# Four 64x64 quadrants for the recurrence of a hybrid trunk, a 16x16 block inverse, and shape changes in the planner's costs

## The chip, the cores and the metric

The kernel runs on one core of a Trainium2 chip. A core has TensorE (128 x 128 array, PE in the profile; its weight loads are PEld), VectorE (DVE), ScalarE (ACT), GpSimd (POOL) and SyncE (SP, which issues the transfers). Matrix products read SBUF and write PSUM, which has eight banks of 512 fp32 columns on 128 partitions. The metric is the device time of one execution in microseconds (us), the median of several; lower is better.

## The reference

A trunk of four residual layers on x of 256 tokens x 1024 channels, fp32. Layers 0 and 3 mix tokens with RWKV-7, layer 1 with stick-breaking attention, layer 2 with sparse attention over keys that an indexer selects; a SwiGLU network follows each. The change concerns RWKV-7 (16 heads of 64 channels), whose core is a recurrence over tokens:

```python
def step(state, inp):                      # state: 64 x 64 for each head
    r_t, w_t, k_t, v_t, kk_t, a_t = inp
    sa = jnp.einsum('bhvk,bhk->bhv', state, kk_t)
    state = (state * w_t[:, :, None, :]
             - sa[..., None] * (kk_t * a_t)[:, :, None, :]
             + v_t[..., None] * k_t[:, :, None, :])
    return state, jnp.einsum('bhvk,bhk->bhv', state, r_t)
...
y = ((y - mu) * lax.rsqrt(var + RW_GN_EPS)).reshape(B, S, D) * ln_w + ln_b
y = y + (jnp.sum(rh * kh * r_k, axis=-1, keepdims=True) * vh).reshape(B, S, D)
out = (y * g).astype(h.dtype) @ w_out
```

## The kernel before, in words

Activations lie with channels on partitions: 1024 channels are 8 groups (index p, NC = 8) of 128 partitions, two heads in each. `halves` lists for the two heads hh of a group their own 64 partitions r and the other 64, rb. Functions work on two neighbouring groups at a time, which I call a pair of groups.

The recurrence is cut into chunks of C = 64 tokens, NCH = 4 of them. Inside a chunk it is linear algebra on 64 x 64 blocks for each head. The steps and the names of their buffers, which the profile shows as out<-in:

- `sc`: products of keys and queries of a chunk, masked into SB (strict part for the inverse, the other part for the output).
- the inverse of a unit lower triangular 64 x 64 matrix for each head and chunk. First its two 32 x 32 diagonal blocks are inverted by forward substitution on VectorE: all 256 blocks lie along partitions and the free axis (`blocks`, `inv`), and 31 iterations of a multiply and a subtract each handle 31 to 256 elements a partition. A transposed copy goes to XT. Then `combine` makes the off-diagonal 32 x 32 block with two TensorE units of 16 tiny products (`cmb1`, `cmb2`) for each pair of groups; `xd` is a transposed copy of XT that it needs.
- `vp`: the product that makes the values, 128 single fp32 products of 256 columns over both layers, ends in `vfirst`. `qct`: transposes of keys. `vtok`: values turned to tokens on partitions and centred, into UV. `bv`: SB times UV, the part of the right-hand side that does not depend on the state.
- `bn`: sums over a head's channels by a product with a block matrix of ones (`bonesr`), in two products of split fp32 (`prhl`, split by `exact`).
- `pg`: the gate.
- `Chain`: one for each pair of groups, two of them alternate, for groups 0 to 3 and then 4 to 7. A step c does: pS = state times PR (four 64x64 products); u = pS + BV on VectorE; Y<-PR,Sn (the state's part of the output); xu = XT times u; UV = -xu (scaling on ScalarE or VectorE); qu = QC times UV (K = 128, four products of 128 x 64 tiles); the new state Sn = (qu) dc + (Sp dc), the second term made as Sd; Y<-SB,UV (K = 128).
- `post`: the output's group norm, and `po`, the output projection.

A head's products use the 64 x 64 part of the array with rows r (or rb) and columns r: two heads of a group take two of the four quadrants.

The order of the work is not the order of the code. A `Plan` records every operation; `unit(at_once, ns)` binds TensorE products into one piece of work with a given cost. A list scheduler (`_schedule`) then sets for each engine the order, by ranks from the longest remaining path, by a table of perturbations of ranks (`NUDGES`) and by a cost `SWITCH` for a change between products that use half the array or less and whole-array products. Where TensorE would stand idle, `keep_warm` inserts bf16 products into an unused bank (`warm_o`, "warmers"). Operations of queue `anye` may go to ScalarE or VectorE. All recorded instructions are issued from one helper line (L788 before, L808 after); the warmers have their own (L1893, L1933). `bank` takes one of the PSUM banks, `t1` and `t2` take rotating SBUF buffers of 256 and 512 columns.

The core of the substitution:

```python
for i in range(31):
    shape = [P, 31 - i, i + 1]
    ...
    dve.tensor_tensor(t, a, b, op=ALU.mult)
    dve.tensor_tensor(XI[:, i + 1:, :i + 1], XI[:, i + 1:, :i + 1], t, op=ALU.subtract)
```

Of the kernel before, what the change touches and what calls it, by code (L numbers as in the profile page):

```python
# [22 lines left out]
P = 128  # L23
# [14 lines left out]
LAST = 4  # L38
NEG = -1.0e30
# [21 lines left out]


# [118 lines left out]
class Op:  # L181


    def __init__(self, eng):
        self.eng, self.instrs, self.cost, self.table, self.cols = eng, [], 0.0, None, 0.0
        self.preds, self.succs, self.alts, self.warmer, self.parts = set(), [], {}, False, False
# [68 lines left out]
SWITCH = 95.0  # L255
# [53 lines left out]
class Plan:  # L309
# [37 lines left out]
    def record(self, eng, method, args, kw):  # L347
# [19 lines left out]
        if eng == "tensor":  # L367
            op.cols += _columns(method, outs[0], ins)
            op.parts = outs[0].p1 - outs[0].p0 <= 64 or ins[0].p1 - ins[0].p0 <= 64
# [101 lines left out]
    def _schedule(self, counts, reserve):  # L471
        engines = ("tensor", "vector", "scalar", "gpsimd", "sync")
        ready, pending, free = ({e: v() for e in engines} for v in (list, list, float))
        out, recent, parts = [], collections.deque(), False
# [68 lines left out]
        def keep_warm(t, until):  # L543

            nonlocal parts, hot
# [14 lines left out]
            t, parts = t + (SWITCH if parts else 0.0), False  # L560
# [25 lines left out]
        def choose(e, t):  # L586
# [3 lines left out]
            while ready[e] and got is None:  # L590
# [17 lines left out]
                if watch and o.parts != parts and held is None and not o.alts:  # L608
                    held = item, r[1]
                    skipped.append(item)  # L610
                    continue
                if held and (o.parts != parts or o.rank < held[0][2].rank - STICK):
# [20 lines left out]
        while done < len(self.ops):  # L633
# [132 lines left out]
    def emit(self, nc, counts, warmer):  # L766
# [12 lines left out]
        for k in sorted(first, key=lambda k: size[k] % 128 > 0):  # L779
            first[k].get()  # L780
# [11 lines left out]
def trunk(ctx: ExitStack, tc: tile.TileContext, xT_in, vecs_in, wts, lora_in, consts_in, id32_in, nqk_in, outT, order, layers=None):  # L792
# [42 lines left out]
    def consts0():  # L835
        load_consts(0)
        pool.tensor_copy(identb, cst("ident"))
        anye.copy(bonesr, cst("bones"))
# [10 lines left out]
    bonesr = T([P], name="bonesr", dtype=F32R)  # L849
# [53 lines left out]

    def exact(out, w, x, hl):

        split(hl[0], hl[1], x)
        with unit():
            pe.matmul(out, w, hl[0], start=True, stop=False)
            pe.matmul(out, w, hl[1], start=False, stop=True)
# [182 lines left out]
    def rwkv(j, layer, after):  # L1092
# [119 lines left out]
        for p in range(0, NC, 2):  # L1212
            pw = bank("lw"), bank("la")
            with unit(2, 960.0):
# [59 lines left out]
        for p in range(0, NC, 2):  # L1274
# [5 lines left out]
            am = t2("am")  # L1280
            for q in range(2):
                anye.affine(am[:, q], Ft[:, p + q, :], vec(f"ka{j}", p + q), omka[:, j, p + q:p + q + 1])
            dve.tensor_tensor(Et[:, p:p + 2], am, di, op=ALU.mult)
            dve.tensor_tensor(Ft[:, p:p + 2], Ft[:, p:p + 2], di, op=ALU.mult)
# [36 lines left out]
        for p in range(NC):  # L1321
            o = bank("sc"), bank("sc")
            with unit(2):
# [8 lines left out]
        room = T([2, 1024], "s0", "blocks")  # L1332
        ct_ = room[:, 0].rearrange("p (t k a c) -> p t k a c", t=32, k=2, a=4)
        for k in range(2):
            for g in range(4):
                r, b = slice(g * 32, (g + 1) * 32), g % 2
                anye.copy(ct_[r, :, k].rearrange("p t a c -> p a c t"), SB[k][r, g // 2, :, :, 0, b * 32:(b + 1) * 32])
        inv = T([2, 32, 32], "s7", "inv")
        dve.transpose(flat(inv[:, 0]), ct_.rearrange("p t k a c -> p (t k a c)"))
        sp.dma_start(inv[:, 1], id32_in)  # L1340
        ab_, XI = inv[:, 0], inv[:, 1]
        xtmp = room[:, 1, :S]
        for i in range(31):
            shape = [P, 31 - i, i + 1]
            t = xtmp[:, :(i + 1) * (31 - i)].rearrange("p (a b) -> p a b", a=31 - i)
            a = ab_[:, i + 1:, i:i + 1].to_broadcast(shape)
            b = XI[:, i:i + 1, :i + 1].to_broadcast(shape)
            dve.tensor_tensor(t, a, b, op=ALU.mult)
            dve.tensor_tensor(XI[:, i + 1:, :i + 1], XI[:, i + 1:, :i + 1], t, op=ALU.subtract)

        XT = [T([16, C], t, "XT") for t in ("wh", "wl")]
        for k in range(2):
            anye.memset(XT[k], 0.0)
        ct_ = room[:, 0].rearrange("p (t k u) -> p t k u", t=32, k=2)
        dve.transpose(ct_.rearrange("p t k u -> p (t k u)"), flat(inv[:, 1]))
        for k in range(2):
            for g in range(4):
                r, b = slice(g * 32, (g + 1) * 32), g % 2
                anye.copy(XT[k][r, :, b * 32:(b + 1) * 32], ct_[r, :, k].rearrange("p t u -> p u t"))
# [38 lines left out]
        for p in range(0, NC, 2):  # L1398
            o = bank("qct"), bank("qct")
            with unit(2, 560.0):  # L1400
# [9 lines left out]
        for p in range(0, NC, 2):  # L1410
            Vp = vfirst[p // 2]
            o = bank("vtok")
            with unit(1, 990.0):
                for q in range(2):
                    for c in range(NCH):
                        for hh, r, rb in halves:
                            pe.matmul(o[rb, q * S + c * C:q * S + (c + 1) * C], Vp[r, q, c * C:(c + 1) * C],
                                      cst("center")[r, hh * 64:hh * 64 + 64], start=True, stop=True)
            for hh, r, rb in halves:
                anye.copy(UV[hh][rb, p:p + 2].rearrange("p n c t -> p (n c) t"), c8(o[rb, :]))  # L1420
            o = bank("bv")
            with unit(1, 980.0):
                for q in range(2):
                    for c in range(NCH):
                        for hh, r, rb in halves:
                            pe.matmul(o[r, q * S + c * C:q * S + (c + 1) * C], SB[p // 4][rb, hh, p % 4 + q, c, 0, :],
                                      UV[hh][rb, p + q, c, :], start=True, stop=True)
            anye.copy(pairs(BV, p), c8(o))


        for p in range(0, NC, 2):
            prs = t2("prs")
            for q in range(2):
                anye.scale(prs[:, q], pr[:, p + q], vec(f"rk{j}", p + q))
            bn = bank("bn")
            exact(bn, bonesr, flat(prs), [flat(t2("prhl", F32R)) for _ in range(2)])
            dve.tensor_tensor(pr[:, p:p + 2], ab(bn), vfirst[p // 2], op=ALU.mult)
# [14 lines left out]
        def combine(p):  # L1452

            X = XT[p // 4][:, (p % 4) * NCH:(p % 4 + 2) * NCH]
            xd = flat(t2("xd"))
            dve.transpose(xd, flat(X))
            z, zs, z2 = bank("cmb1"), t1("zs"), bank("cmb2")
            with unit(1, 540.0):
                for c in range(2 * NCH):
                    for lo in (0, 64):  # L1460
                        hi = lo + 32
                        pe.matmul(z[hi:hi + 32, c * 32:(c + 1) * 32], SB[p // 4][lo:hi, lo // 64, p % 4 + c // NCH, c % NCH, 0, 32:],
# [595 lines left out]
```

## Time and profile before

| | value |
|---|---|
| median of 3 runs | 1368.67 us (1368.57 to 1369.37) |
| profiled execution, its own time | 1368.04 us |
| its span in the profile | 1366.2 us |
| TensorE busy | 1357.6 us (99%) |
| VectorE busy | 1124.7 us (82%) |
| ScalarE busy | 796.0 us (58%) |
| transfers | 220.07 MB, mean 161 GB/s |
| granted TensorE clock | 1.000 |

The span is the time from the first to the last instruction in the profile; 1.8 us of the execution's time lie around it. A group's row reads: line, engine, operation, out<-in, tile of the array, partitions x elements, type, count of records, then busy time and mean duration in ns, then the idle time of the engine before them and what ended most of it. A timeline row reads: start, duration until the last of the row ended, and then the same names.

Where the two RWKV layers' work of this change lies: in layer 0 from about 76 us (`sc`) to 150 us, in layer 3 at about 1050 us and after.

### The profile page before, as it was taken

What the parts mean: (1) busy time and instruction counts of PE and PEld (TensorE: products, weight loads), DVE (VectorE), ACT (ScalarE), POOL (GpSimd) and SP (SyncE); (2) the same over time, 40 slices, a digit from 0 to 9 for tenths busy, and PEclk for the clock granted to TensorE, in tenths of its full rate; (3) what the DMA queues carried; (4) which work ended last, traced back from release to release, by engine and by line L of the source; (5) the groups of instructions that cost most, each with busy time, mean ns of one, the idle gap of its engine ahead of it and who ended that gap; (6) DMA issues with size and microseconds to landing.
All of it is one profiled execution on the core that took longest, in us unless ns stands there. A gap on an engine that the chain in (4) does not pass through costs nothing.

```text
span 1366.2 us, 25568 instructions
## 1 busy us (share of the span) xinstructions
PE 1357.6 (99%) x10202; PEld 1189.5 (87%) x10202; DVE 1124.7 (82%) x1954; ACT 796.0 (58%) x1342; POOL 12.2 (1%) x18
## 2 busy tenths in 40 slices
PE   9999999999999999999999999999999999999998
PEld 8988898888888898888887798888899888988887
DVE  8999689886677788886679998887599996888864
ACT  7966755454455765544455965554388366665542
POOL 0100000000000000000000000000000000000000
PEclk9999999999999999999999999999999999999999
DMA  6423156555655345655654445556544231656553
GB/s 243 149 84 119 44 175 198 187 187 180 193 175 153 126 151 186 191 194 196 210 183 139 163 137 187 185 187 198 185 123 130 77 108 51 184 184 188 187 190 116
DMA packets 61335, 220.07 MB, mean 161 GB/s; under 512 B 6816, under 2 KB 8352, under 8 KB 60960
## 3 DMA queue, kind: packets, MB, share of 16 engines
q1 hardware_dynamic: 61216, 218.44, 50.2%
q8 instruction: 80, 1.31, 0.4%
q14 instruction: 39, 0.32, 0.1%
HBM read 217.36 MB, written 1.05 MB: 160 GB/s over the span
## 4 chain that ended last, share of the span: by engine, by line
PE 92%; DVE 6%; DMA 1%; issue 1%; ACT 0%; SPq 0%; DVEq 0%; ACTq 0%
PE dn L788 18%; PE gate L788 18%; PE up L788 18%; PE po L788 7%; PE qk L788 3%; PE vps L788 3%; PE rp L788 3%; PE kp L788 2%; PE z L788 2%; PE vp L788 2%; PE q L788 2%; PE k L788 2%; PE Y L788 1%; DVE blocks L788 1%; PE sc L788 1%; PE attn_o L788 1%
## 5 line engine op out<-in xcount | busy, mean ns | idle before, releaser
L788 ACT CAST wh<-raw 128x1024 fp32r<-128x1024 f32 x350 | 366.3, 1050 | 343.7 <-PE dn L788 110.1
L788 DVE TENSOR_TENSOR wl<-raw,wh 128x1024 fp32r<-128x1024 f32 x383 | 461.6, 1221 | 76.8 <-ACT wh L788 69.6
L788 PE MATMUL gate<-xg,wh 128*128 128x512 f32 x704 | 263.4, 392 | 0.0
L788 PE MATMUL up<-xg,wh 128*128 128x512 f32 x704 | 262.7, 392 | 0.0
L788 PE MATMUL dn<-h,wh 128*128 128x512 f32 (+1 forms) x720 | 246.3, 389 | 0.0
L788 PE MATMUL dn<-h,wl 128*128 128x256 f32 x704 | 197.2, 280 | 0.0
L788 PE MATMUL gate<-xg,wl 128*128 128x256 f32 x704 | 197.1, 280 | 0.0
L788 PE MATMUL up<-xg,wl 128*128 128x256 f32 x704 | 197.1, 280 | 0.0
L788 PEld LDWEIGHTS dn<-h,wh 128*128 128x128 f32 x720 | 134.0, 188 | 30.0
L788 PEld LDWEIGHTS up<-xg,wh 128*128 128x128 f32 x704 | 131.7, 187 | 28.8
L788 PEld LDWEIGHTS gate<-xg,wh 128*128 128x128 f32 x704 | 131.7, 187 | 28.6
L788 PEld LDWEIGHTS gate<-xg,wl 128*128 128x128 f32 x704 | 133.0, 189 | 0.1
L788 PEld LDWEIGHTS up<-xg,wl 128*128 128x128 f32 x704 | 133.1, 189 | 0.1
L788 PEld LDWEIGHTS dn<-h,wl 128*128 128x128 f32 x704 | 132.8, 189 | 0.0
L788 ACT CAST h<-gus 128x512 fp32r<-128x512 f32 x43 | 26.7, 621 | 53.0 <-DVE gus L788 52.9
L788 PE MATMUL vp<-xv,raw 128*128 128x256 f32 x256 | 57.3, 382 | 0.3 <-PE qct L788 0.3
L788 DVE TENSOR_TENSOR gus<-gus,rstd 128x512 f32<-128x512 f32 x88 | 57.2, 684 | 0.2
L788 PEld LDWEIGHTS vp<-xv,raw 128*128 128x128 f32 x256 | 48.0, 190 | 7.7 <-issue 0.7
L788 DVE TENSOR_TENSOR h<-gus,h 128x512 fp32r<-128x512 f32 x44 | 30.4, 691 | 24.8 <-ACT h L788 24.8
L788 PE MATMUL rp<-prx,wh 128*128 128x256 f32 x256 | 49.7, 295 | 0.0
L788 PE MATMUL kp<-kx,wh 128*128 128x256 f32 x256 | 48.4, 288 | 0.5 <-DVE kx L788 0.4
L788 PE MATMUL po<-yhl,wh 128*128 128x256 f32 x256 | 48.3, 289 | 0.0
(331 smaller groups left out, 2432.2 us busy)
## 6 DMA issues: line engine op xcount, KB each, us to landing
raw<-in_wts_dram SPq DMA_DIRECT2D x401, 512.0 KB, 3.9
lora<-in_lora_dram SPq DMA_DIRECT2D x2, 1280.0 KB, 9.7
xt<-in_xT_dram SPq DMA_DIRECT2D x4, 256.0 KB, 4.0
lora<-in_lora_dram SPq DMA_DIRECT2D x2, 512.0 KB, 5.3
inv<-in_id_dram SPq DMA_DIRECT2D x2, 512.0 KB, 3.6
out_dram<-xt SPq DMA_DIRECT2D x8, 128.0 KB, 2.9
sbt<-in_consts_dram SPq DMA_DIRECT2D x1, 512.0 KB, 3.9
consts<-in_consts_dram SPq DMA_DIRECT2D x1, 288.0 KB, 5.8
```

Source lines behind the costliest of these rows:

```text
L788: getattr(getattr(nc, o.eng), method)(*map(real, args), **{k: real(a) for k, a in kw.items()})
```

## The change

1. A constant `SWAP` exchanges the two 64-channel halves of the value channels in groups 2, 3, 6 and 7. It is applied on the host to the columns or rows of the weights that make or use values (g2, the value projection, v2, v0, the group norm's vectors, the output projection's rows). In those groups the values of head hh therefore lie on partitions rb while its keys lie on r.
2. `four(p0)` lists eight products for four groups; for the first pair the value side is e = r, for the second e = rb, so that four consecutive products use four quadrants. They write two banks, one for each pair. vtok, bv, bn and the products of the recurrence with K = 64 are issued in this way, for four groups instead of two.
3. There is one `Chain` for four groups. Its units have eight products; pS, xu and qu become three slots of the two banks `chain`. Y<-SB,UV is split: the part of the values goes into one opening unit of 32 products, the part of u stays in the step. The state is Sn = (b + Sp) dc with two VectorE operations over a pair of groups in place of Sd and a fused multiply-add for each group.
4. The forward substitution runs on 16 x 16 blocks: 15 iterations, a multiply and a subtract each, of 30 to 128 elements. The 32 x 32 inverses are completed by two TensorE units of 128 tiny products each (`cmb0`) with a copy and four scalings, and by more transposes. `combine` handles four groups at a time and reads the transposed blocks directly, so that `xd` goes.
5. bn is an fp32 product with ones on 64 x 64 quadrants instead of two products of a split operand; `bonesr` and `exact` go.
6. In the preparation of Et and Ft (EF) one multiply over 1024 elements replaces two over 512.
7. The planner keeps the tile shape of a unit's first and last product (`op.shape`) and charges SWITCH plus `ENTER` for each change of shape; costs of units (`sc`, `qct`, `pv`, `z`, `lw`, `idx`) and the table NUDGES are new. `LAYOUT` keeps the order in which buffers are placed in SBUF.

The products change in number from 800 of 64 x 64 or 128 x 64 tiles to 832 on four quadrants and 96 of 128 x 64, both layers together; of the tiny 32 x 32 ones from 256 to 256 plus the 512 of `cmb0`.

The diff, cut:

```diff
+SWAP = np.array([c ^ (64 * (c // 256 % 2)) for c in range(D)])
...
-    (461406, 4825, 4945, 1000), (222252, 5820, 5870, 3000), (292571, 81, 131, 1000), (91922, 1777, 1897, 1000),
+    (156698, 2078, 2128, 3000), (802374, 350, 650, 300), (387552, 1920, 1928, 3000), (301531, -118, 182, 1000),
...
-SWITCH = 95.0
+SWITCH = 97.0
+WHOLE = (4, 4)
+ENTER = {(2, 4): 100.0, (1, 4): 100.0, (4, 2): 48.0, (2, 2): 48.0, (1, 1): 18.0, (4, 1): 18.0}
...
-                if o.parts != parts:
-                    parts, cost = o.parts, cost + SWITCH
+                if o.shape[0] != shape:
+                    cost += SWITCH + o.enter
+                shape = o.shape[1]
...
-            dve.tensor_tensor(Et[:, p:p + 2], am, di, op=ALU.mult)
-            dve.tensor_tensor(Ft[:, p:p + 2], Ft[:, p:p + 2], di, op=ALU.mult)
+            ef = EF[:, :, p:p + 2]
+            dve.tensor_tensor(ef, ef, di[:, None].to_broadcast([P, 2, 2, S]), op=ALU.mult)
...
-        for i in range(31):
+        for i in range(15):
+            shape = [P, 2, 15 - i, i + 1]
...
+        z = bank("cmb0")
+        with unit(1, 1050.0):
+            for m in range(32):
+                for g in range(4):
+                    r, b, u = slice(g * 32, (g + 1) * 32), g % 2, m % 16
+                    pe.matmul(z[r, 16 * m:16 * m + 16], SB[m // 16][r, g // 2, u // 4, u % 4, 0, b * 32:(b + 1) * 32], half[r, m],
+                              start=True, stop=True)
+        zs = t2("zs0")
+        anye.copy(flat(zs), z)
...
+        def four(p0):
+
+            for q in range(2):
+                for i in range(2):
+                    for hh, r, rb in halves:
+                        yield i, q, p0 + 2 * i + q, hh, r, rb, rb if i else r
+
+        for p0 in range(0, NC, 4):
+            o = bank("vtok"), bank("vtok")
+            with unit(1, 960.0):
+                for c in range(NCH):
+                    for i, q, p, hh, r, rb, e in four(p0):
+                        pe.matmul(o[i][rb, q * S + c * C:q * S + (c + 1) * C], vfirst[p // 2][e, q, c * C:(c + 1) * C],
+                                  cst("center")[e, e.start:e.stop], start=True, stop=True)
...
-            exact(bn, bonesr, flat(prs), [flat(t2("prhl", F32R)) for _ in range(2)])
+            with unit(1, 870.0):
+                for i in range(2):
+                    for hh, r, rb in halves:
+                        pe.matmul(bn[i][rb if i else r], ones[r, :64], flat(prs[i])[r], start=True, stop=True)
...
-                            for hh, r, rb in halves:
-                                pe.matmul(a[r, q * C:(q + 1) * C], PR[r, p0 + q, c, 0, :], Sp[r, q, :],
-                                          start=True, stop=True)
-                    dve.tensor_tensor(u0, ab(a[:, :2 * C]), BV[:, p0:p0 + 2, c], op=ALU.add)
+                        for i, q, p, hh, r, rb, e in four(p0):
+                            pe.matmul(a[i][e, q], PR[r, p, c, 0, :], Sp[i][r, q, :], start=True, stop=True)
+                    for i in range(2):
+                        dve.tensor_tensor(u0[i], a[i], BV[:, p0 + 2 * i:p0 + 2 * i + 2, c], op=ALU.add)
...
-                            sd = t1("Sd")[:, :C]
-                            anye.scale(sd, Sp[:, q], dq)
-                            dve.scalar_tensor_tensor(Sn[:, q], aq, dq, sd, op0=ALU.mult, op1=ALU.add)
+                        if c:
+                            dve.tensor_tensor(Sn, b[i], Sp[i], op=ALU.add)
+                        dve.tensor_tensor(Sn, Sn if c else b[i], d, op=ALU.mult)
...
-            ch = [Chain(4 * half + 2 * i) for i in range(2)]
+            ch = Chain(4 * half)
             for c in range(NCH):
-                for a in ch:
-                    a.step(c)
+                ch.step(c)
```

Three places show what moves. First TensorE in the chain of the first RWKV layer; a row is line, operation, out<-in, the output's size and how many in a row (an fp32 product is one instruction here). Before, units of four from two chains alternate with combine's units:

```order
L788 MATMUL pS<-Sn,PR 64x64 x4
L788 MATMUL qu<-UV,QC 64x64 x4
L788 MATMUL Y<-PR,Sn 64x64 x4
L788 MATMUL xu<-u_1806,XT 64x64 x4
L788 MATMUL cmb_1824<-xd,SB 32x32 x16
L788 MATMUL pS<-Sn,PR 64x64 x4
L788 MATMUL Y<-SB,UV 64x64 x4
```

After, units of eight from the chains of both halves stand there (chain<-Sn,PR is pS, chain<-u,XT and chain<-QC,XT are xu, chain<-UV,QC is qu; the x32 is the second half's opening unit):

```order
L808 MATMUL Y<-SB,UV 64x64 x8
L808 MATMUL chain<-Sn,PR 64x64 x8
L808 MATMUL Y<-SB,UV 64x64 x32
L808 MATMUL chain<-u_2185,XT 64x64 x8
L808 MATMUL chain<-QC,XT 64x64 x8
L808 MATMUL Y<-PR,Sn 64x64 x8
L808 MATMUL chain<-UV,QC 64x64 x16
L808 MATMUL Y<-SB,UV 64x64 x8
```

Each of the products of 64 x 64 tiles now stands in a run of at least eight of one shape, and the second half's chain is among the first's.

Second, TensorE where the inverse's result is wanted, in the same layer. Before:

```order
L788 MATMUL qct<-consts_98,QC 128x64 x32
L788 MATMUL vtok<-consts_98,vf_115 64x64 x16
L788 MATMUL vp<-xv,raw_1164 128x256 x2
L788 MATMUL bn<-prhl,bonesr 128x512 x4
L788 MATMUL vtok<-consts_98,vf_114 64x64 x16
L788 MATMUL vtok<-consts_98,vf_116 64x64 x16
L788 MATMUL bv<-UV,SB 64x64 x64
```

After:

```order
L808 MATMUL vp<-xv,raw_1170 128x256 x2
L808 MATMUL vp<-xv,raw_1221 128x256 x2
L808 MATMUL cmb_1260<-blocks,SB 32x16 x128
L808 MATMUL qct<-consts_98,QC 128x64 x48
L808 MATMUL vp<-xv,raw_1170 128x256 x2
L808 MATMUL vp<-xv,raw_1221 128x256 x2
L808 MATMUL vtok<-consts_98,vf_112 64x64 x2
```

The first unit of tiny products comes between the last products of vp, ahead of vtok; the vtok products of two buffers alternate.

Third, VectorE after the inverse. Before, a transpose, the copies to XT, and the transposes into xd:

```order
L788 STREAM_TRANSPOSE blocks<-inv 128x1024
L788 TENSOR_TENSOR pr<-bn,vf_113 128x512
L788 COPY XT<-blocks 32x16x32 x4
L788 STREAM_TRANSPOSE xd<-XT 128x512
L788 COPY XT<-blocks 32x16x32 x2
L788 TENSOR_TENSOR wl_1601<-raw_1343,wh_1424 128x1024
L788 STREAM_TRANSPOSE xd<-XT 128x512 x2
```

After, two transposes, and with other work between them three of the four scalings of the second tiny unit's result and the last transpose:

```order
L808 STREAM_TRANSPOSE blocks<-inv 128x16x32
L808 STREAM_TRANSPOSE blocks<-inv 128x32x32
L808 TENSOR_TENSOR wy<-raw_1239,wy 32x1024
L808 TENSOR_TENSOR wl_1389<-raw_1243,wh_1258 128x1024
L808 COPY QC<-qct 128x8x64 x2
L808 COPY UV<-vtok 64x512 x3
L808 TENSOR_SCALAR blocks<-cmb_1540 16x32x16 x3
L808 TENSOR_TENSOR pr<-bn,vf_115 128x512
L808 STREAM_TRANSPOSE blocks<-blocks 128x1024
```

The copies to XT and combine come behind that last transpose.

More of the change, by code (lines that the diff above doesn't have):

```diff
@@ L607, in choose @@
                     continue
-                if watch and o.parts != parts and held is None and not o.alts:
+                if watch and o.shape[0] != shape and held is None and not o.alts:
                     held = item, r[1]
@@ L1322, in rwkv @@
             o = bank("sc"), bank("sc")
-            with unit(2):
+            with unit(2, 900.0):
                 for c in range(NCH):
@@ new lines, in rwkv @@
+        zs = t2("zs0")
+        anye.copy(flat(zs), z)
+        z = bank("cmb0")
+        with unit(1, 1050.0):
+            for m in range(32):
+                for g in range(4):
+                    r = slice(g * 32, (g + 1) * 32)
+                    pe.matmul(z[g * 32:g * 32 + 16, 16 * m:16 * m + 16], flat(zs)[r, 16 * m:16 * m + 16], W[r, m, 16:], start=True, stop=True)
+        for g in range(4):
+            r = slice(g * 32, g * 32 + 16)
+            anye.scale(W[r, :, 16:], z[r].rearrange("p (m t) -> p m t", t=16), -1.0)
@@ new lines, in rwkv @@
+        for p0 in range(0, NC, 4):
[6 more added lines that the diff above has]
+            for i in range(2):
+                p = p0 + 2 * i
+                for hh, r, rb in halves:
+                    anye.copy(UV[hh][rb, p:p + 2].rearrange("p n c t -> p (n c) t"), c8(o[i][rb, :]))
+            o = bank("bv"), bank("bv")
+            with unit(1, 960.0):
+                for c in range(NCH):
+                    for i, q, p, hh, r, rb, e in four(p0):
+                        pe.matmul(o[i][e, q * S + c * C:q * S + (c + 1) * C], SB[p // 4][rb, hh, p % 4, c, 0, :],
+                                  UV[hh][rb, p, c, :], start=True, stop=True)
+            for i in range(2):
+                anye.copy(pairs(BV, p0 + 2 * i), c8(o[i]))
@@ L1475, in rwkv @@
         class Chain:
             def __init__(self, p0):
-                self.p0, self.Sp = p0, None
-                self.Y = bank("Y", "ps" if p0 >= 4 else "g")
+                self.p0, self.S = p0, None
+                self.W = [bank("chain") for i in range(2)]
+                self.Y = [bank("Y", "ps" if p0 else "g") for i in range(2)]
+                with unit(1, 960.0):
+                    for c in range(NCH):
+                        for i, q, p, hh, r, rb, e in four(p0):
+                            pe.matmul(self.Y[i][e, q * S + c * C:q * S + (c + 1) * C], UV[hh][rb, p, c, :],
+                                      SB[p // 4][rb, hh, p % 4, c, 1, :], start=(c == 0 and q == 0), stop=False)
@@ L1526, in step @@
-                with unit(1, 280.0):
-                    for q in range(2):
-                        for hh, r, rb in halves:
-                            pe.matmul(Y[r, q * S + c * C:q * S + (c + 1) * C], UV[hh][:, p0 + q, c, :],
-                                      SB[p0 // 4][:, hh, p0 % 4 + q, c, 1, :], start=(c == 0 and q == 0),
-                                      stop=(c == NCH - 1 and q == 1))
-                if c == 0:
-                    self.opened = plan.ops[-1]
-                else:
-                    plan.after(plan.ops[-1], [self.opened])
+                    ut = t1("u0").rearrange("p (i a b) -> p i a b", i=2, a=2)
@@ new lines, in step @@
+                    u0 = [ut[:, i] for i in range(2)]
+                    with unit(1, 240.0):
+                        for i, q, p, hh, r, rb, e in four(p0):
+                            pe.matmul(a[i][e, q], PR[r, p, c, 0, :], Sp[i][r, q, :], start=True, stop=True)
+                    for i in range(2):
+                        dve.tensor_tensor(u0[i], a[i], BV[:, p0 + 2 * i:p0 + 2 * i + 2, c], op=ALU.add)
+                    with unit(1, 240.0):
+                        for i, q, p, hh, r, rb, e in four(p0):
+                            pe.matmul(Y[i][e, q * S + c * C:q * S + (c + 1) * C], Sp[i][r, q, :], PR[r, p, c, 1, :],
+                                      start=False, stop=False)
@@ new lines, in step @@
+                with unit(1, 240.0):
+                    for i, q, p, hh, r, rb, e in four(p0):
+                        pe.matmul(u[i][r, q], XT[p // 4][e, (p % 4) * NCH + c, :], u0[i][e, q, :], start=True, stop=True)
+                if c == 0:
+                    plan.after(plan.ops[-1], [self.opened])
+                for i in range(2):
+                    pi = p0 + 2 * i
+                    for hh, r, rb in halves:
+                        anye.scale(UV[hh][r, pi:pi + 2, c, :], u[i][r], -1.0)
@@ L1537, in post1 @@
+                with unit(1, 240.0):
+                    for i, q, p, hh, r, rb, e in four(p0):
+                        pe.matmul(Y[i][e, q * S + c * C:q * S + (c + 1) * C], UV[hh][r, p, c, :],
+                                  SB[p // 4][r, hh, p % 4, c, 1, :], start=False, stop=(c == NCH - 1 and q == 1))
         def post1(p, Y, yhl):
@@ L1603, in pv @@
     def pv(o, v, vcol, ats):
-        with unit(2):
+        with unit(2, 628.0):
             for tb in range(2):
```

227 lines of the change are left out of this document (100 added, 127 removed), and 32 rows, old and new, of the table NUDGES.

## The prediction

> **What bounds the kernel now.** I read the page first: span, engines, clock, and the chain that ended last.
>
> ```profile
> span 1366.2 us, 25568 instructions
> PE 1357.6 (99%) x10202; PEld 1189.5 (87%) x10202; DVE 1124.7 (82%) x1954; ACT 796.0 (58%) x1342; POOL 12.2 (1%) x18
> PEclk9999999999999999999999999999999999999999
> PE 92%; DVE 6%; DMA 1%; issue 1%; ACT 0%; SPq 0%; DVEq 0%; ACTq 0%
> ```
>
> TensorE is busy for 1357.6 of 1366.2 us at full clock, so only 8.6 us of the span are not its own, and the chain is 92% TensorE. The time therefore moves by what the change does to TensorE's work, plus any new wait. Next, the groups by line and shape, for TensorE's products that the change touches (idle time before them at the end of each row):
>
> ```profile
> L788 PE MATMUL vtok<-consts,vf 64*64 64x64 f32 x256 | 8.8, 220 | 0.0
> L788 PE MATMUL bv<-UV,SB 64*64 64x64 f32 x256 | 8.7, 219 | 0.7 <-DVE inv L788 0.5 <-issue 0.2
> L788 PE MATMUL Y<-SB,UV 128*64 128x64 f32 x256 | 14.0, 230 | 0.0
> L788 PE MATMUL Y<-PR,Sn 64*64 64x64 f32 x192 | 10.4, 227 | 0.0
> L788 PE MATMUL pS<-Sn,PR 64*64 64x64 f32 x192 | 10.1, 226 | 0.1
> L788 PE MATMUL qu<-UV,QC 128*64 128x64 f32 x192 | 10.0, 230 | 0.0
> L788 PE MATMUL xu<-u,XT 64*64 64x64 f32 x192 | 10.0, 226 | 0.0
> L788 PE MATMUL xu<-QC,XT 64*64 64x64 f32 x64 | 3.4, 224 | 0.0
> L788 PE MATMUL cmb<-xd,SB 32*32 32x32 f32 x256 | 5.4, 192 | 0.5 <-DVE xd L788 0.4
> L788 PE MATMUL cmb<-XT,zs 32*32 32x32 f32 x256 | 5.4, 192 | 0.3 <-DVE pr L788 0.3
> L788 PE MATMUL bn<-prhl,bonesr 128*128 128x512 f32 x16 | 5.8, 432 | 0.4 <-DVE prhl L788 0.2
> ```
>
> An fp32 product leaves two records, so the first eight rows are 1600/2 = 800 products and the two cmb rows 512/2 = 256. The idle column is nearly zero: in these stages also TensorE waits for almost nothing. Busy times overlap in them, so a price comes from start to start in the timeline (start, busy):
>
> ```profile
> 117.88 1.27 PE L788 MATMUL bn<-prhl,bonesr 128*128 128x512 f32 x4
> 119.08 2.08 PE L788 MATMUL vtok<-consts,vf 64*64 64x64 f32 x64
> 121.00 1.10 PE L788 MATMUL bv<-UV,SB 64*64 64x64 f32 x32
> ...
> 134.94 1.20 PE L788 MATMUL cmb<-XT,zs 32*32 32x32 f32 x64
> 136.07 0.45 PE L788 MATMUL qu<-UV,QC 128*64 128x64 f32 x8
> ...
> 142.66 0.45 PE L788 MATMUL qu<-UV,QC 128*64 128x64 f32 x8
> 143.04 0.69 PE L788 MATMUL cmb<-XT,zs 32*32 32x32 f32 x32
> 143.66 0.45 PE L788 MATMUL xu<-u,XT 64*64 64x64 f32 x8
> 143.94 0.40 PE L788 MATMUL Y<-PR,Sn 64*64 64x64 f32 x8
> 144.18 0.40 PE L788 MATMUL pS<-Sn,PR 64*64 64x64 f32 x8
> ```
>
> vtok: 32 products in 121.00 - 119.08 = 1.92 us, 60 ns each. Y<-PR, between neighbours of its own shape: 4 in 0.24, again 60. qu, with another shape on either side: 4 in 143.04 - 142.66 = 0.38, so a change of tile shape costs 0.14. cmb: 32 in 1.13 and 16 in 0.62; the difference gives 31.9 ns each and 0.11 for the change. Four bn records take 1.20.
>
> How many tiles run at once? These rows tell:
>
> ```profile
> 81.34 2.06 PE L788 MATMUL sc<-PR,QC 64*128 64x128 f32 x32
> 86.37 13.22 PE L788 MATMUL vp<-xv,raw 128*128 128x256 f32 x60
> ...
> 131.69 0.22 PE L788 MATMUL cmb<-xd,SB 32*32 32x32 f32 x2
> 131.71 0.22 PE L788 MATMUL cmb<-XT,zs 32*32 32x32 f32 x3
> ...
> 131.78 0.19 PE L788 MATMUL cmb<-xd,SB 32*32 32x32 f32 x1
> ...
> 1050.74 1.07 PE L788 MATMUL v<-xv,lora 128*32 128x256 f32 x16
> 1051.74 0.51 PE L788 MATMUL rp<-prx,wh 128*128 128x256 f32 x2
> ```
>
> vp on the whole array: 30 products of 256 columns in 13.22, 0.44 each, so about 0.22 at 128 columns. sc, whose two 64-row tiles share all columns, needs 2.06/16 = 0.13 for 128: two row tiles run together. v, four column tiles on all rows, needs 1.00/8 = 0.125 for 256 columns: four run together. Where the two cmb units overlap, four different 32x32 positions are in use: of the twelve records that begin from 131.69 to 131.78, the first rows and the last are shown; eleven steps in 0.09 us are 8 ns a record, 16 a product, half of 31.9. Not shown anywhere: a two-by-two grid of 64x64 tiles, each row of the grid feeding both columns.
>
> **The change, part by part.**
>
> *Four quadrants.* Today a unit's heads sit on two of the four 64x64 quadrants (r to r, or rb to r), 60 ns a product. After, vtok, bv and the products of the recurrence with K=64 use all four. Their number is 128 + 128 + 128 (the opening unit, Y's v-part) + 448 (56 chain units of 8) = 832, because Y<-SB with K=128 becomes two K=64 halves. Bounds: 60 ns if only two run at once, 30 if four do. I take 30, since row tiles (sc), column tiles (v) and four small tiles (cmb) all ran in parallel: 832 x 0.030 = 25.0. The state update b keeps its 96 products of 128x64: 96 x 0.060 = 5.8.
>
> *Inverse.* 512 tiny products (N=16) on four positions are new. Bounds 8 ns (half of the 16, for half the columns) and 31.9 (cmb's ordinary price); I take 16, the fastest rate that rows show: 512 x 0.016 = 8.2. combine's first product now uses four positions: 128 x 0.016 = 2.0; its second stays at 128 x 0.0319 = 4.1.
>
> *bn.* 16 fp32 products, 64x64, N=512 on four quadrants. From v: 0.125 for 256 columns, 0.25 for 512: 4.0, against 4 x 1.20 = 4.8 before (two-at-a-time bound 8.0).
>
> TensorE before: 800 x 0.060 + 256 x 0.0319 + 4.8 = 48.0 + 8.2 + 4.8 = 61.0. After: 25.0 + 5.8 + 8.2 + 2.0 + 4.1 + 4.0 = 49.1. Difference -11.9.
>
> *Shape changes.* Counted in the two orders, runs of one tiled shape fall from 151 to 91 (64x64: 54 to 24; 128x64: 47 to 18). 59 of them at 0.14 less 0.1 for the one more 32x32 run: -8.2. Returns from a tiled run to split whole-array products fall from 44 to 33; their price lies between 0 and the 0.14 of a change, I take 0.09: -1.0.
>
> *Warmers.* These fill TensorE's expected waits.
>
> ```profile
> L1893 PE MATMUL warm_o<-warm_x 128*128 128x256 bf16 x60 | 11.2, 342 | 1.2 <-DVE eps_gn L788 1.2
> 137.07 0.83 PE L1893 MATMUL warm_o<-warm_x 128*128 128x256 bf16 x6
> 137.83 0.45 PE L788 MATMUL pS<-Sn,PR 64*64 64x64 f32 x8
> ```
>
> Six take 0.76, 0.127 each. In the two recurrence stages they fall from 26 to 18: -1.0. At the start they rise from 34 to 38, inside the wait for the first weights: nothing; without that cover, 0.5.
>
> *Waits that go.* bv's wait for the inverse (0.5 in its group) and cmb's for xd (0.4): -0.95 with rounding. The inverse on VectorE:
>
> ```profile
> 92.37 0.20 DVE L788 TENSOR_TENSOR blocks<-inv 128x31 f32<-128x31 f32 x1
> ...
> 122.41 0.18 DVE L788 TENSOR_TENSOR inv<-inv,blocks 128x31 f32<-128x31 f32 x1
> ```
>
> 62 operations, with others between, take 30 us. After, 30 shorter ones: at most 30 x 0.49 = 14.5. What follows them (transposes, a tiny unit, a copy, a tiny unit, four scalings, transposes, copies to XT) is VectorE and ScalarE work of some 10 us, and the first unit waits for it. The cover is vp, two runs of 13.2 us like the row at 86.37, and qct, vtok and bv behind: I cost it at nothing. If the cover fails, the combine units and with them the chain stand up to 5 us late.
>
> *EF, bn's split, xd.* The broadcast multiply replaces two; 16 split operations and 8 xd transposes go. VectorE is not the bound, these sit under TensorE: nothing, at most 0.5 either way.
>
> *The chain's waits.* One Chain now carries four pairs, so its steps no longer alternate between two independent chains. Today's latencies of a step:
>
> ```profile
> 138.32 0.29 DVE L788 TENSOR_TENSOR u<-pS,QC 128x128 f32<-128x128 f32 x1 [0.15 <-PE pS L788]
> 139.35 0.56 ACT L788 ACTIVATE UV<-xu 64x128 f32<-64x128 f32 x2
> 143.23 0.47 DVE L788 SCALAR_TENSOR_TENSOR Sn<-qu,dc,Sd 128x64 f32<-128x64 f32 x2 [0.16 <-PE qu L788]
> ```
>
> A step pS, u, xu, UV, qu, Sn is today about 3.3 us of latency; after, two u additions and four Sn operations of 0.29 in line make about 4.1. In the new order the first layer has five dependent steps, since the second half starts beside the first, and the last layer four: 9 x 4.1 = 37 us of latency in stretches that hold some 45 us of TensorE work, pg, the openers, combine and po among it. So most is covered, not all: bounds 0 and 9 (1 us a step); I take 2.5, near today's end, because today's rows leave TensorE idle by 0.1 there.
>
> Sum: -11.9 - 8.2 - 1.0 - 1.0 - 0.95 + 2.5 = -20.55. The profiled execution took 1368.04 (its span and 1.8 around it, which the change leaves); 1368.04 - 20.55 = 1347.5. The median of the runs, 1368.67, is 0.6 above it: **1348.1, so 1348**.
>
> **Rivals.**
> R1, slower: only two of the four 64x64 quadrants run at a time, because the tiles of one unit contend for banks or weight loads. Place: all 832 products and bn. Price: 832 x 0.030 + 4.0 = 29.0, giving 1377.1. It decides once a product costs 30 + 30 x 20.55/29.0 = 51 ns. For it: no row shows the two-by-two grid, and both row tiles write into one bank, in two pairs. Against: today's pS also writes one bank from two row tiles, and 60 ns is about half of the 110 that vp's 0.44 us for 256 columns makes of 64.
> [...]
>
> R2: a floor of 31.9 ns a product. Then 832 x 1.9 + 128 x 15.9 + 512 x 15.9 ns = 1.6 + 2.0 + 8.1 = 11.7 more: 1359.8. For it: 31.9 is what all long runs of small tiles show. Against: the overlapped units at 16.
> [...]
>
> R3: the steps bind; every one of nine leaves TensorE idle 1 us: 9 instead of 2.5, so 1354.6. For it: the longer step and one chain instead of two. Against: the work named above.
>
> R4: the tiles gain nothing here and the waits eat the switches: within 0.2% of before.
>
> **Chances and range.** Forecast 0.74, R3 0.12, R2 0.06, R1 0.06, R4 0.02. The range 1341 to 1361 takes in R3 and R2; its low end has the inverse at 8 ns (-4.1) and no chain wait (-2.5). 0.2% (2.7 us) is about what a measurement here tells from no change. Faster 0.92, same 0.02, slower 0.06.
>
> **What would show it.** In the new profile: vtok's 64 products of a unit in 1.9 us (R1: 3.8); chain units of 8 within 0.25; the tiny units of 128 in about 2.0 (R2: 4.1); TensorE busy some 22 us less with idle time up by 2 to 3, on the rows of chain and Y; no wait on inv before bv. Wrong would be: quadrant products at 60 ns, idle time of 5 us or more behind UV or Sn, or a wait for the tiny units' copies.

## The result, and the profile after

The changed kernel takes 1384.05 us (median of 6 runs, 1382.21 to 1387.91), the kernel before 1368.62 (6 runs): a ratio of 1.0115, 95% interval 1.010 to 1.013. It is slower by 15 us; the forecast was 1348. The profiled execution took 1382.43. The page of the changed kernel, with the rows that answer to those of before:

```profile
span 1380.4 us, 28055 instructions
PE 1349.3 (98%) x11494; PEld 1180.5 (86%) x11494; DVE 1101.0 (80%) x1887; ACT 773.8 (56%) x1294; POOL 9.9 (1%) x22
PEclk9998999999999999999999999999999999999999
q8 instruction: 90, 1.47, 0.4%
```

TensorE's busy time fell by 8.3 us only, not by 22, and its idle time rose from 8.6 to 31.1 us. The last row is from the table of transfers: a queue of the kind "instruction" moved 90 packets, 1.47 MB. That is 16 KB a packet, and 22988 matmul and weight-load records make 255 of them a packet. Before, the row was

```profile
q8 instruction: 80, 1.31, 0.4%
```

with 20404 records, again 255 a packet. No view names the engine that this queue serves; that it brings TensorE its instructions is read from this ratio. An fp32 product, which the lists of the order count once, takes four instructions: vtok's unit of 64 products leaves 128 weight-load and 128 matmul records.

The waits of TensorE (engine, what waited, releaser: us in all, times, longest) say what the idle time is:

```profile
PE cmb L808 <- issue: 10.1, 4, 3.6
PE chain L808 <- issue: 5.0, 4, 1.9
PE vp L808 <- issue: 1.6, 1, 1.6
PE Y L808 <- issue: 1.2, 3, 0.6
PE bv L808 <- issue: 0.4, 1, 0.4
PE bn L808 <- issue: 0.4, 1, 0.4
```

"issue" means that the engine waited for nothing that the profile shows. They sum to 18.7 us; before it was 0.2. The timeline of the first RWKV layer shows where:

```profile
111.18 1.84 PE L808 MATMUL cmb<-blocks,SB 32*32 32x16 f32 x198
116.58 0.81 PE L808 MATMUL cmb<-blocks,SB 32*32 32x16 f32 x58 [3.56 <-issue]
...
122.08 2.10 PE L808 MATMUL vtok<-consts,vf 64*64 64x64 f32 x128
124.11 1.33 PE L808 MATMUL cmb<-blocks,zs 32*16 32x16 f32 x142
127.92 1.14 PE L808 MATMUL cmb<-blocks,zs 32*16 32x16 f32 x114 [2.47 <-issue]
128.99 1.99 PE L808 MATMUL bn<-prs,ones 64*64 64x512 f32 x8
...
143.04 0.46 PE L808 MATMUL chain<-QC,XT 64*64 64x64 f32 x16
143.33 1.04 PE L808 MATMUL bn<-prs,ones 64*64 64x512 f32 x8
144.30 0.69 PE L808 MATMUL chain<-UV,QC 128*64 128x64 f32 x16
145.58 0.46 PE L808 MATMUL chain<-Sn,PR 64*64 64x64 f32 x16
145.97 0.75 PE L808 MATMUL cmb<-blocks,SB 32*32 32x32 f32 x64
...
156.29 1.03 PE L808 MATMUL chain<-UV,QC 128*64 128x64 f32 x28 [1.94 <-issue]
```

In bursts the four quadrants do nearly what was forecast: vtok's 64 products take 124.11 - 122.08 = 2.03 us, 32 ns each. A chain unit of eight takes 143.33 - 143.04 = 0.29 us next to its own tile shape, where 0.25 was forecast, and 145.97 - 145.58 = 0.39 with a change of shape. The tiny products too run at about 17 ns each (198 records in 1.84 less 0.18 of the last one's length). But a unit of 128 of them breaks off after 99 and stands for 3.56 us, the second one after 71 for 2.47. After such a gap the same bn unit takes 1.99 us instead of 1.04. The windows (stretch, us; busy time and records of PE, PEld, DVE, ACT, POOL; granted clock; share of the transfer engines; GB/s) say why:

```profile
92.00:131.00 39.00, 32.97 (x798) 28.06 (x797) 18.79 (x46) 12.64 (x21) 0.00 (x0) 0.91 0.41 135
131.00:165.00 34.00, 29.45 (x986) 24.64 (x984) 21.77 (x56) 17.78 (x47) 2.28 (x4) 0.91 0.16 50
1100.00:1140.00 40.00, 33.32 (x1088) 26.98 (x1088) 24.54 (x45) 18.62 (x36) 2.56 (x4) 0.96 0.27 83
```

Windows of 0.5 us show the clock at 1.00 or at 0.50, and a value between only where it changes (0.87 at 116.5 to 117, 0.50 from there to 120, 0.72 at 120 to 120.5, 1.00 after). So it was at half for 2 x (0.09 x 39 + 0.09 x 34 + 0.04 x 40) = 16 us, which costs up to 8 us, an estimate from these windows. Windows of 2 us show 0.50 at 118 to 120, 128 to 132 and 158 to 160 us, each time shortly after one of the three long gaps of the rows above, the second of which has 0.50 already at 127.25 to 127.5; before it was 1.00 in all three stretches.

### The profile page after: what moved, and what is told of

It is laid out like the page before. It is cut to its first block, busy times and chain, and to the rows that moved or that the text cites. A ratio compares the mean times of both kernels' runs of the same rounds, so it can differ in the third digit from the quotient of the medians.

```text
span 1380.4 us, 28055 instructions
## 1 busy us (share of the span) xinstructions
PE 1349.3 (98%) x11494; PEld 1180.5 (86%) x11494; DVE 1101.0 (80%) x1887; ACT 773.8 (56%) x1294; POOL 9.9 (1%) x22
## 3 DMA queue, kind: packets, MB, share of 16 engines
q8 instruction: 90, 1.47, 0.4%
## 4 chain that ended last, share of the span: by engine, by line
PE 95%; DVE 2%; issue 2%; ACT 1%; DMA 0%; SPq 0%; DVEq 0%; ACTq 0%
PE dn L808 18%; PE up L808 18%; PE gate L808 18%; PE po L808 7%; PE vp L808 4%; PE rp L808 3%; PE kp L808 3%; PE qk L808 3%; PE vps L808 3%; PE z L808 2%; PE k L808 2%; PE q L808 2%; PE cmb L808 1%; PE chain L808 1%; PE sc L808 1%
## 5 line engine op out<-in xcount | busy, mean ns | idle before, releaser
L808 ACT CAST wh<-raw 128x1024 fp32r<-128x1024 f32 x354 | 369.8, 1050 | 322.4 <-issue 107.7
L808 PE MATMUL po<-ohl,wh 128*128 128x256 f32 x256 | 48.2, 288 | 0.0
```

The lines of the kernel that those rows point to most:

```text
L808: getattr(getattr(nc, o.eng), method)(*map(real, args), **{k: real(a) for k, a in kw.items()})
```

## The experiments

Theory A: TensorE's instructions come in blocks of 256, about 3.5 us apart at best (the queue of instructions moved 3 of its packets in the 7.0 us from 1111.2 to 1118.2 of the changed kernel, 8 in the 26 us from 114 to 140), and the tiny units and the quadrants use them up faster. I call the rate at which they come the supply, and what has come and is not yet issued the block in hand. Rivals: the four quadrants contend over long streams; data or transfers in the trunk are late.

**The streams alone.** A kernel of TensorE streams without transfers beside them: `quads(w, 384, x, QUADS[:2])`, which is 384 products of 64 x 64 on two quadrants, `quads(four, 384, x, QUADS)` on four, 384 tiny ones, 768 in bf16, and units of 32 between whole-array products (`mixed`).

> Not the trunk: TensorE streams alone, set apart by 24 whole-array products each. 384 fp32 products on two 64x64 quadrants, 384 on four, 384 tiny ones (32x16x16) on four positions, 768 bf16 on four quadrants, then 12 times (32 on four quadrants, 4 whole-array products of 256 columns). No transfers run beside them. Theory A (TensorE's instructions come in blocks of 256, one every 3.4 us at best as the trace of the changed kernel shows them, and an fp32 product takes four): two quadrants 60 ns a product, as before; four quadrants 32 ns for the first 70 to 120 products and 53 on average after, with gaps of 1 to 3 us, about 18 us for the stream; tiny about 18 us too; bf16 with two instructions a product about 27 ns, 20 us; the mixed stream without gaps, its 384 products at 32 ns. Theory B (four tiles contend with each other over long streams): 60 ns a product on four quadrants without gaps, 23 us, and the mixed stream as slow. Theory C (the waits in the trunk come from its data or its transfers): no gaps here, four quadrants 12 us, tiny 4 to 6, bf16 12.

Its timeline (w with 64x64 is the stream on two quadrants, w with 128x512 the separators):

```profile
35.99 22.61 PE L41 MATMUL w<-x 64*64 64x64 f32 x768
58.53 20.87 PE L35 MATMUL w<-x 128*128 128x512 f32 x48
79.33 3.72 PE L41 MATMUL four<-x 64*64 64x64 f32 x239
84.57 2.09 PE L41 MATMUL four<-x 64*64 64x64 f32 x128 [1.52 <-issue]
88.02 2.09 PE L41 MATMUL four<-x 64*64 64x64 f32 x128 [1.36 <-issue]
92.03 2.09 PE L41 MATMUL four<-x 64*64 64x64 f32 x128 [1.91 <-issue]
...
100.15 20.87 PE L35 MATMUL w<-x 128*128 128x512 f32 x48
120.95 1.74 PE L53 MATMUL tiny<-x 32*16 32x16 f32 x191
124.67 1.25 PE L53 MATMUL tiny<-x 32*16 32x16 f32 x128 [1.99 <-issue]
...
139.97 22.97 PE L35 MATMUL w<-x 128*128 128x512 f32 x48
162.87 2.44 PE L41 MATMUL bfour<-xb 64*64 64x64 bf16 x271
...
180.30 21.58 PE L35 MATMUL w<-x 128*128 128x512 f32 x48
201.81 1.16 PE L41 MATMUL mixed<-x 64*64 64x64 f32 x64
202.90 1.99 PE L35 MATMUL w<-x 128*128 128x256 f32 x8
```

This is one execution. Theory A's pattern is there, with other sizes: the four quadrants take 20.8 us where some 18 were expected, bf16 17.4 where 20 were. Two quadrants: 22.5 us, 59 ns a product, no gap. Four: 239 records run through, then bursts of exactly 128 matmul records (256 with their loads), one every 3.4 to 4.0 us: 20.8 us for 384 products, 54 ns. That mean takes in the first 120 products, which were in hand; after them 64 products come every 3.4 to 4.0 us, 54 to 63 ns each. Tiny: 19.0 us, 50 ns, though a burst of 128 records takes 1.25 us there and not 2.09. bf16, two instructions a product: 17.4/768 = 23 ns. And 32 products on four quadrants between longer work run at 1.09/32 = 34 ns with no gap.

The mean granted clock was 1.00 over the stream on four quadrants, 0.57 over the tiny one and 0.65 over the bf16 one, and the bursts came at the same pace in all three, one in 3.4 to 4.0 us, so the clock does not set that pace. The quadrants did not contend (a burst's 64 products in 2.09 us, 33 ns each, where two quadrants take 59), and the gaps came without transfers or late data (the transfer engines' share was 0.02 over the bf16 stream, and no wait of the three streams is for data). A stream of 384 fp32 products takes 50 to 54 ns each, and the supply alone, with nothing left in hand, gives hardly more than the one product in 60 ns that two quadrants use. Whether transfers lengthen a gap is not shown: the longest gap is 2.48 us here and 3.56 in the changed kernel, whose transfer engines were 0.75 busy during it, and no run varied them.

**The 32x32 substitution back.** `for i in range(31)` on VectorE in the changed kernel in place of the 16x16 one; `cmb0` with its copy and scalings goes.

> The changed kernel with the 32x32 substitution of before on VectorE (31 iterations) in place of the 16x16 one; the 512 tiny products, their copy, scalings and one transpose go, all else stays. Theory A (instruction supply): 2048 fewer TensorE instructions; the 10.1 us of waits before cmb go, 8 us of work go, and most of the 17 us at half clock: 1350 to 1362. Theory B (the four quadrants are at fault): the waits on chain, Y and bv stay and only the 8 us of work go: about 1376. Theory C (data too late): the longer substitution on VectorE delays the chain further: 1384 or more.

Measured: 1375.76 us, ratio 1.0057 (1.0042 to 1.0072). Below the changed kernel by 8.3, but a miss for theory A's number; theory B's, about 1376, is met. The waits before cmb are gone and the profiled execution's clock is 0.999, as theory A has it; waits for issue of 8.3 us stay, on chain, Y, bv and vtok, as theory B has it. So this run does not decide between the two. The timeline tells what spoils it as a test: from the first `sc` to the last `po` of a layer the two RWKV layers take 109.4 + 115.1 us, against 111.5 + 118.6 before and 120.2 + 119.0 after, so 14.7 us less than in the changed kernel there; everything else takes 1149.0 against 1141.2, 7.8 us more, 4.1 of them ahead of the first layer's `sc`. The scheduler had made another order in all stages, which its table NUDGES was not made for. An edit that is planned anew tells two things at once.

**The 16x16 inverse alone in the kernel before.** Two units of tiny products, nothing else of the change.

> The kernel before with the change's 16x16 inverse alone (two units of 128 tiny products, a copy, four scalings, more transposes); combine, the chains and everything else as before. Theory A: the units stall as they do in the changed kernel: 8 us of work, some 7 to 10 us of waits for instructions and some at half clock, 1383 to 1395. Theory B (quadrants at fault, the tiny units only work): 8 us more, 1377. Theory C (the shorter substitution is worth something): 1365 or less.

Measured: 1413.63, ratio 1.0329 (1.0312 to 1.0346), 45 us slower. Its waits of TensorE name the same cause (the row below, from the list of waits), but this order too is new: outside the two layers it loses 17 us (1153.4 against 1136.1), inside 28.4, which is more than theory A's upper end. The clock over the two layers, 0.96 in the first and 0.94 in the second, accounts for up to 13 us of the 28.4, an estimate from the time at that clock.

```profile
PE cmb L788 <- issue: 10.5, 4, 5.0
```

**Y in one product.** The 32x32 substitution and `UV[hh][:, p, c, :]` (K = 128) instead of two halves.

> As the kernel with the 32x32 substitution, and also Y<-SB,UV in one product of K = 128 (128x64 tiles, 60 ns) instead of two of K = 64 on four quadrants: 128 products fewer, the opening units go; the same array time. Theory A: 512 fewer instructions, two blocks: 3 to 7 us below the kernel with the 32x32 substitution alone, 1346 to 1357. Theory B (quadrants at fault): as much or a little faster, since fewer products use them. If neither supply nor quadrants bind there: the same within 1 us.

Measured: 1373.38, ratio 1.0041 (1.0026 to 1.0056): 2.4 us below its counterpart, a little under the 3 expected, and far above the level of 1346 to 1357; again planned anew, so weak.

**The same order, fewer instructions.** A cleaner test leaves the changed kernel's order as it is on every engine and replaces only what a unit issues:

```diff
+        plan.ops[-1].short = [("matmul", (z[g * 32:(g + 1) * 32, 16 * m:16 * m + 64], ...,
+                                          half[g * 32:(g + 1) * 32, m:m + 4].rearrange("p m t -> p (m t)")), ...)
+                              for m in range(0, 32, 4) for g in range(4)]
...
-            for method, args, kw in o.instrs:
+            for method, args, kw in getattr(o, "short", o.instrs):
```

> The changed kernel in its own order, every row of every engine as it was, but each unit of 128 tiny products is issued as 32 products of 64 columns on the same four positions into the same bank (about the same array time, 1 us a unit; the inverse is not computed rightly): 1536 TensorE instructions fewer. Theory A (instruction supply): the 10.1 us of waits in front of cmb go, and most of the 17 us at half clock that follow such waits (8 us of work at most): 1362 to 1370. Theory B (the tiny units are innocent, the chain and its quadrants lose the time): 1380 to 1384.

Measured: 1364.17, ratio to before 0.9969 (0.9959 to 0.9979): 19.9 us below the changed kernel, as theory A had it. Its page begins:

```profile
span 1360.4 us, 26519 instructions
```

Its waits of TensorE:

```profile
PE chain L808 <- issue: 4.5, 3, 2.4
PE Y L808 <- issue: 2.4, 3, 1.5
PE bv L808 <- issue: 0.9, 1, 0.9
PE pg L808 <- issue: 0.9, 1, 0.9
PE bn L808 <- issue: 0.6, 1, 0.6
```

And its windows over the first RWKV layer, the same two stretches as above:

```profile
92.00:131.00 39.00, 35.63 (x747) 30.62 (x747) 26.25 (x61) 17.88 (x32) 2.22 (x4) 1.00 0.39 132
131.00:165.00 34.00, 28.60 (x829) 22.70 (x824) 22.71 (x61) 18.50 (x50) 0.06 (x1) 1.00 0.19 52
```

The waits before cmb are gone and the clock is 1.00 in both. One thing besides the count differs: a short unit takes 1.03 us (from 110.71 to 111.74 in the timeline), where 128 products at 17 ns make 2.2. So some 4 to 5 of the 19.9 us are less work for the array and not supply; with these put back, some 1368 to 1369 lies in theory A's range still, and not in theory B's. Waits for issue of 9.3 us remain in and around the chain, where small products follow each other.

**Two quadrants in the same order**, with `yield ..., r` for both pairs of groups (and r to r in bn):

> The changed kernel in its own order, but all eight products of a unit of the recurrence, of vtok, bv and bn on two quadrants (r to r) as in the kernel before; the same count of instructions (values of every second pair of groups are wrong). By array time alone it loses 832 x 0.030 + 4 = 29 us: 1413. Theory A: the supply gives one product in 53 us/1000, so two quadrants at 60 cost only where the block in hand would have let four run at 31: 1390 to 1403. Theory B (four quadrants never helped): 1384.

**and with the short units:**

> Both edits together, the order still the same: tiny units in 32 products and only two quadrants. Against the one with the short units alone it shows what the four quadrants are worth when the tiny units take no supply. Theory A: 15 to 25 us above that one, more than the step from the changed kernel to the one with two quadrants. Array time alone: 29 us in both. Theory B: no difference.

Measured: 1392.96 (ratio 1.0183, 1.0168 to 1.0198) and 1372.23 (1.0028, 1.0017 to 1.0039). So the four quadrants are worth 8.9 us with the long tiny units and 8.1 without: neither 29 nor 0. The first fits theory A; the 15 to 25 expected of the second are a miss: I had thought that the tiny units take most of the supply, but with four quadrants the chain exhausts it by itself. With two quadrants and short units the waits of TensorE for issue are nearly gone:

```profile
PE Y L808 <- issue: 0.6, 1, 0.6
PE chain L808 <- issue: 0.5, 1, 0.5
```

The profiled executions of the two runs with short units are 10.6 us apart. TensorE is busy for 22.7 us more with two quadrants (1361.1 against 1338.4) and idle for 12.1 less (9.9 against 22.0); 8.2 of the 12.1 are waits for issue, 3.4 are waits for data and buffers. Why the busy time differs by 22.7 and not by 29 is not shown.

**The whole computation in the changed kernel's order.** Could the 19.9 us be had without leaving work out? Here the 62 operations of the 32x32 substitution take the place of the 30, the order of all other rows is written into the program, and the tiny units go.

> The changed kernel with the 32x32 substitution on VectorE as in the earlier experiment of that kind, but with the changed kernel's own order written into the program (every other row of every engine stands where it stood; the 62 operations take the place of the 30; the tiny units are gone), so that no planning differs. Theory A (instruction supply): as the kernel with short tiny units, and some 4 us less since those units' array time goes too: 1357 to 1362, below the kernel before; the earlier 1375.8 then came from its new order. If the longer substitution comes too late (rival): 1366 or more, with waits on XT or cmb for VectorE.

Measured: 1379.3, ratio 1.0082 (1.0068 to 1.0095): the rival's time, though its waits are on bn and vp and not on XT or cmb. VectorE is late, and the mean granted clock is 0.993 again. Two of its waits:

```profile
PE vp L987 <- issue: 9.5, 2, 8.3
PE bn L987 <- DVE QC L987: 4.5, 1, 4.5
```

The 8.3 us "issue" stands in the last layer beside the row of 62 operations in VectorE's queue, ahead of the work that frees vp's banks; the trace names no releaser for it. It ends at 1099.29 us, 0.1 after VectorE's first `vf<-vd,vp` there, which stands behind the first half of the substitution; so it is most likely a wait for vp's bank and not for instructions. With Y whole:

> As the kernel with the 32x32 substitution in the changed kernel's order, and Y<-SB,UV in one product of K = 128 per head and chunk (60 ns) instead of two halves on four quadrants (31 ns each): equal array time, 512 TensorE instructions fewer in the chain. Theory A: the supply still binds in the chain there, so 2 to 6 us below that kernel: 1352 to 1358. If the supply binds nowhere any more: the same within 1 us.

Measured: 1372.7, ratio 1.0032 (1.0020 to 1.0043), 6.6 below; the step is slightly over the expected one, but the level of 1352 to 1358 is missed. The waits for issue on chain and Y fall by only 1.9 us (from 4.2 to 2.3), so most of this step is not shown to be the supply. Then the operations spread over VectorE's queue:

> As the kernel with the 32x32 substitution in the changed kernel's order, but its 62 operations are spread over VectorE's queue from where the substitution begins to where the last transpose of blocks stood, instead of standing in a row; there they held up what was queued behind them (QC, vfirst) for 4.5 and 8.3 us. Theory A (instruction supply, with those VectorE waits as that run's only loss): 1357 to 1363. If VectorE's queue still holds TensorE up: 1366 or more with waits on QC, UV or vfirst.

> The same, with Y<-SB,UV whole (K = 128), 512 TensorE instructions fewer. In the order with the operations in a row this was worth 6.6 us. Theory A: again 3 to 6 us below its counterpart: 1352 to 1358. If the supply binds only where VectorE is late: within 1 us of it.

Measured: 1369.28 (ratio 1.0001, 0.9992 to 1.0010) and 1367.96 (1.0000, 0.9987 to 1.0014): as fast as before, not faster, no step clear of noise between the two, and a miss for both of theory A's numbers. In the first of the two, the first layer is now 107.7 us against 111.5 before; the last, 116.0 against 118.6, is held up by VectorE, as a wait shows:

```profile
PE vtok L987 <- DVE vf L987: 4.8, 1, 4.8
```

In its groups by line (busy us, mean ns, idle us before them) the substitution stands as two:

```profile
L987 DVE TENSOR_TENSOR inv<-inv,blocks 128x31 f32<-128x31 f32 (+15 forms) x62 | 21.2, 342 | 1.8
L987 DVE TENSOR_TENSOR blocks<-inv 128x31 f32<-128x31 f32 (+15 forms) x62 | 21.2, 341 | 1.7
```

The 32x32 substitution keeps VectorE busy for 21 us a layer (42.4 in both). What these two layers gain, 6.4 us, the rest of the span takes back, 7.4 (1143.5 against 1136.1; the changed kernel itself has 1141.2 there). No version tried that does the whole computation beats the kernel before. One that spreads the tiny products between vp's was not tried.

## Why the prediction was wrong, point by point

- The step that failed is "How many tiles run at once?" and the prices drawn from it. 30 ns for a quadrant product and 16 for a tiny one are right as rates of the array, and the changed kernel's rows show 32 and 17. As prices over a stage they are wrong: I took a rate seen over twelve records for one that 512 products can hold. The bound "31.9 (cmb's ordinary price)" was too low as well; a stream of 384 takes 50 to 54 each.
- R2 was the right kind of rival, a floor, with the wrong size: 31.9 ns instead of 54, and I argued it away with the overlapped units. A floor of 54 applied as R2 was would add 832 x 24 + 128 x 38 + 128 x 22 + 512 x 38 ns = 47 us, 1395. The measured 1384 lies between that and the forecast, as it should if blocks in hand let the short bursts run.
- The row that speaks of it was there: the page of before has a queue of instructions with 80 packets, and I did not read it. The kernel before ran its quadrant products at 60 ns, just above the floor.
- R1 gave the right sign by a mechanism that is not there: the four quadrants do not contend (streams alone: bursts of 128 records in 2.09 us).
- The rest of the sum comes out where the supply does not bind. With short tiny units and two quadrants the forecast's 1348.1 + 29.0 makes 1377.1; the four short units took 4.1 us where 8.2 was costed, which leaves 1373.0, against a measured 1372.2. That holds for the sum as a whole: shape changes, warmers and waits were not measured singly, and their errors may cancel. What is missing from the 1384.05, some 36 us, is shown in two steps: 19.9 by the tiny units, of which 4.1 is their work and 15.8 their instructions and the half clock that follows; and of the quadrants' 29 us only 8.1 came, which is 20.9 short.
- "If the cover fails, the combine units ... stand up to 5 us late": the cover of vp did hold in the first layer. TensorE had 60 of the layer's 64 vp products done ahead of the first tiny unit at 111.18 us, the transposes that this unit reads had ended at 104.5, and no wait on inv is left.
- The chain's waits for data were small: 1.2 + 0.5 + 0.5 + 0.3 + 0.2 = 2.7 us on chain and Y, near the 2.5 taken and far from R3's 9.
- The shorter substitution stands in the sum only by the waits that go. In the changed kernel's order it is worth more in the last layer, where VectorE is full from the substitution to the chain: with the longer one, spread, vtok waits 4.8 us for values that VectorE copies, where the changed kernel waits 0.4.
- Not explained: some 2.6 us in the first feed-forward layer (184.4 us from the last `po` to the first `qk` before, 187.0 after), with the same records. The forecast had put everything outside the two layers at nothing. The rest of the 5.1 us that the changed kernel takes longer there (1141.2 against 1136.1) lies ahead of the last layer's first `sc`, where 27 more records of `rp` stand: work moved and not lost.

## What to carry to other kernels

Count instructions as well as columns: the streams of small fp32 products were bounded by the supply of TensorE's instructions, 256 every 3.4 to 4.0 us and four to a product, so that making each product faster than some 54 ns gained only in bursts shorter than the block in hand. Small products belong between long ones, as the mixed stream ran at 34 ns a product without a gap; a substitution on another engine may be cheaper than 512 products that take 17 ns each, if that engine has the time (1369.28 with the 32x32 one spread, 1384.05 in the changed kernel). And to test one cause in a scheduled kernel, keep the order fixed and change what a unit issues: the same edits planned anew mixed in 8 to 17 us outside the two layers.

## What the runs showed of the hardware that was not expected

- The supply: after a first run of 191 to 271 matmul records, bursts of exactly 128 and gaps of 1.4 to 2.5 us, in the streams on four quadrants, of tiny products and of bf16, with no transfer of data beside them. A burst and its weight loads are 256 instructions, which agrees with the 255 records that each of the 90 packets of 16 KB stands for; the waits for issue were 18.7 us in the changed kernel and 0.2 before.
- A gap cost twice: bn took 1.99 us instead of 1.04 behind one of 2.47. The granted clock was 0.50 in windows of 2 us behind gaps of 1.94, 2.47 and 3.56 us, with thin work around them. Not each gap has this: in the run with short units a gap of 2.42 us in the chain, at 146.10 us, left the clock at 1.00. What decides it is not shown.
- Four positions of the array ran together in both forms tried in fp32: 64x64 at 32 ns a product, tiny ones at 17.
